# A hybrid decoder layer on one core: the down-projection's split inputs in the activations' pool, the second norm's row asked for later

## The chip, the core and the metric

The kernel runs on one core of a Trainium2 chip. The core has TensorE (PE: matmuls, with weight loads on a sequencer row of their own, PEld), VectorE (DVE), ScalarE (ACT), GpSimd (POOL) and SyncE (SP), which run side by side and wait for each other by semaphores; 16 DMA engines move data between HBM and the on-chip buffer. The metric is the device time of the one launch in microseconds; the median of three runs before is 2255.06 (2254.88 to 2256.31).

## The reference

One layer of a decoder trunk, sequence 512, model width 2048, feed-forward width 6144, everything in fp32. After an RMSNorm one input projection feeds three groups of heads (a pooling mixer, a gated DeltaNet, an RG-LRU); their outputs are joined and projected. What matters here is what follows:

```python
x = x + mixed @ w_out                       # 2048 x 2048
h = rmsnorm(x, norm2_w)
up = h @ w_up                               # 2048 x 12288
gate, val = jnp.split(up, 2, axis=-1)
gate = causal_dwconv(gate, conv_w)          # width 3
x = x + (jax.nn.gelu(gate) * val) @ w_down  # 6144 x 2048
return rmsnorm(x, final_norm_w)
```

`rmsnorm(x, w)` is `x * rsqrt(mean(x * x) + 1e-6) * w` over the 2048 features of a token.

## The kernel before

**Split products.** TensorE takes fp32 operands in a rounded form (`F32R`). To keep fp32 accuracy each operand is held as a rounded part `hi` and a rest `lo`, and each product is three matmuls into one sum: `hi*hi`, `hi*lo`, `lo*hi` (`mm3`, L198 to L203; so the three lines L201, L202 and L203 are the three passes). `parts` (L272) makes such a pair: a cast on ScalarE, a subtraction on VectorE. Activations lie feature by feature, 128 features on the partitions and the 512 tokens along the free axis, so they are the streamed operand; the weights (128x1024 fp32 a tile, 512 KB) come by DMA into `raw` and are split into `whi` and `wlo`.

**Two pools.** The pool `ap_` holds 32 tiles `ah0` to `al15` of 128x512 fp32: the split inputs `xh`, `xl` of the input projection (`ps_u`), then `yh`, `yl` of the out-projection (`ps_o`). As those are done, `act_tile` (L807) takes the tiles in turn from a list `free` for the up-projection. The pool `ep` of the feed-forward holds tags `r1` (two buffers), `r3`, `acc0` to `acc15`, and `ea0` to `ea11`.

**Up-projection.** The 2048 x 12288 product is done for each of 48 pairs of 128 gate and 128 value columns as a Strassen-like scheme: seven products (`b11`, `t1`, `b22`, `t2`, `b21`, `t3`, `t4`), each of 8 x 3 matmuls of 256 columns on one of seven *forms* of the activations. `fa` is the first form (a11: half of the features, half of the tokens; eight tiles made by `first_block`); `fb` holds two more; `fs` holds four sums of blocks (`split_sums`, L823: for six of the eight feature tiles in `ea0` to `ea11`, for the last two in tiles of `ap_`). The 336 products are sorted into slots; in slot n the weights of slot n + 3 are split, and loads run seven slots ahead. Weights of one chain are added up by DMAs on POOL's queue that accumulate onto the raw tile (L1172). The first slots are, in order: b11 of pair 0, b11 of pair 1, t1 of 0, b21 of 0, b22 of 0, t2 of 0, t1 of 1, t3 of 0. Sums are combined by ACT copies and DVE additions (`stage`, from L1199); `e` (L1213 after t2, L1217 after t3) is the DVE addition that reads bank `ps_y`, onto which the pair's next product in that bank writes.

**The second norm.** Its row of `1/rms` is not needed by the products, only by their results. The squares of the last out-projection features are added to `ssum` in slot 1 (`squares`, L866), and `last_squares` then spawns the coroutine `norm2`. A coroutine that yields a number is taken up again when the kernel's own count of PE's time, `now`, has moved on by so many microseconds; `token_rstd` (L160) first does four matmuls `ps_n` of `ssum` against ones, then a chain of 4-column operations on DVE (`ms_n` to `rt_n`, L170 and L130 to L135), yields 3.5, and then does four matmuls `n_ps` that spread the row over the partitions, and an ACT copy into `rstd` (L177).

**Down-projection.** The results `gelu(gate) * value` went to DRAM by pairs; `g_load` brings two of them back, `g_split` (L954) splits them into `gs` tiles. The 48 pairs are taken two at a time, each for two halves of the output features: a chunk is eight sums `ps_d` of 2 x 3 matmuls of 512 columns, each added to `accd` by DVE (L1007). The last two chunks are done by halves of 256 tokens (`ps_e`, L1086 and around), with the final norm's squares in 256-column tiles `sq3` (L1087) and the output's scaling after it.

**What sets the order.** From the end of the out-projection on, VectorE, ScalarE and GpSimd run in the order in which the code is written (`manual_schedule`); PE and SP do so everywhere. A tile of a tag waits for the last reader of the tile that lay there before.

`HK` = 8 is the number of feature tiles in half of the model width, `G` = 2 that of the inputs in a chunk.

Of the kernel before, what the change touches and what calls it, by code (L numbers as in the profile page):

```python
# [8 lines left out]
F32 = mybir.dt.float32  # L9
F32R = mybir.dt.float32r  # L10
# [8 lines left out]
P = 128  # L19
S = 512  # L20
# [42 lines left out]
G = 2  # L63
# [16 lines left out]
class Body:  # L80
# [704 lines left out]
    def out_phase(self):  # L785
        tc, nc, io = self.tc, self.nc, self.io
        with ExitStack() as ctx:
            pool = lambda name, **k: ctx.enter_context(tc.tile_pool(name=name, **k))
            g2 = pool("g2", bufs=1)
            ep = self.ep = pool("ffn", bufs=1)  # L790
# [3 lines left out]
            for p in range(HK):  # L794
                t = ep.tile([P, 2, S], F32, tag=f"acc{2 * p}", name=f"xp{p}")
# [6 lines left out]
            self.forms = {f: [None] * HK for f in BLOCKS + SUMS}  # L802
            free = [f"{t}{n}" for n in range(KT) for t in ("ah", "al")]
            tt = nc.vector.tensor_tensor
            st = {}

            def act_tile(name, shape):  # L807

                return self.ap_.tile(shape, F32R, tag=free.pop(0), name=name)

            def sums(p):

                big = p == HK - 1
                xs = ep.tile([P, 2, S], F32, tag="acc12" if big else "r3", name=f"xs{p}")
                for i in range(2):
                    nc.scalar.activation(xs[:, i, :], res(p + 8 * i), AF.Copy, scale=self.prm("n2", p + 8 * i))
                t = st[p] = ep.tile([P, 4, HT], F32, tag="acc8" if big else "r1", name=f"st{p}", bufs=1 if big else 2)
                a11, a21, a12, a22 = xs[:, 0, 0:HT], xs[:, 0, HT:S], xs[:, 1, 0:HT], xs[:, 1, HT:S]
                tt(out=t[:, 1, :], in0=a21, in1=a22, op=ALU.subtract)
                tt(out=t[:, 2, :], in0=t[:, 1, :], in1=a11, op=ALU.subtract)  # L820
                tt(out=t[:, 3, :], in0=t[:, 2, :], in1=a12, op=ALU.add)
                tt(out=t[:, 0, :], in0=a11, in1=a21, op=ALU.subtract)
# [17 lines left out]
            def split_block(x, h, l, d):  # L840
                nc.scalar.activation(h, x, AF.Copy, scale=self.prm("n2", d))
                nc.vector.scalar_tensor_tensor(out=l, in0=x, scalar=self.prm("n2", d), in1=h.bitcast(F32),
                                               op0=ALU.mult, op1=ALU.subtract)

            def first_block(p):
                t = act_tile(f"fa_{p}", [P, 2, HT])
                split_block(res(p)[:, 0:HT], t[:, 0, :], t[:, 1, :], p)
                self.forms["a11"][p] = t[:, 0, :], t[:, 1, :]
# [26 lines left out]
                        split_sums(d - HK)  # L875

            def norm2():
                yield 5.0
                yield from self.token_rstd(ssum, g2, "n2", rstd)

            for n in range(2):
# [39 lines left out]
            for i in range(2):  # L921
                out_done(DORD[KT - 2 + i], last[i])
            first_block(HK - 1)
            up.split(3)
            sums(HK - 1)
# [13 lines left out]
            gh, gl, wd, graw = {}, {}, {}, {}  # L939
# [9 lines left out]
            def g_load(j0):  # L949
                graw[j0] = ep.tile([P, G, S], F32, tag="r3", name=f"graw{j0}")  # L950
                for i in range(G):
                    nc.sync.dma_start(out=graw[j0][:, i, :], in_=up.gd[j0 + i])

            def g_split(j):  # L954
                j0, i = j // G * G, j % G
                odd = j0 // G % 2
                t = ep.tile([P, 2, S], F32R, tag=("r1", f"ea{i}")[odd], name=f"gs{j}", bufs=(2, 1)[odd])
                self.parts(graw[j0][:, i, :], t[:, 0, :], t[:, 1, :])
                gh[j], gl[j] = t[:, 0, :], t[:, 1, :]

            raws = {}

# [23 lines left out]
            for c, (j0, half) in enumerate(chunks[:-2]):  # L986
                ds = first[8 * (c % 2):8 * (c % 2) + 8] if c < 2 else range(8 * half, 8 * half + 8)
                for i, d in enumerate(ds):
# [11 lines left out]
                    pl, tag = (self.mm, "mm") if d % 2 else (self.aux, "aux")  # L1000
# [13 lines left out]
            j0 = NFF - G  # L1014
            wl = [wd[c - 1], wd[c]]
            HS = S // 2
# [1 line left out]
            s3 = g2.tile([P, 2, HS], F32, tag="ssum", name="ssum3")  # L1018
            r3 = g2.tile([P, 2, HS], F32, tag="rstd", name="rstd3")

            pts, norm_row = {}, {}
            AFTER = 9

            def sums(t, parts, last=False):
# [30 lines left out]
            def scale(t, e):  # L1055

                sl = slice(t * HS, (t + 1) * HS)
                a = acc[e][:, sl]
                if e < ND_:
                    nc.vector.scalar_tensor_tensor(out=a, in0=a, scalar=self.prm("nf", e), in1=norm_row[t][:, 0:HS],  # L1060
                                                   op0=ALU.mult, op1=ALU.mult)
                else:
                    nc.gpsimd.tensor_tensor(out=a, in0=a, in1=r3[:, t, :], op=ALU.mult)
                if e % 2:
                    nc.sync.dma_start(out=io["outT"][:, e - 1:e + 1, sl], in_=acc2[e // 2][:, :, sl])

            for t in range(2):
                sl = slice(t * HS, (t + 1) * HS)
                late, ps8, n8 = [], {}, 8 if t == 0 else 0

                def part(d, i):
                    hi, lo = wl[d // 8][i]
                    wsl = slice((d % 8) * P, (d % 8) * P + P)
                    self.mm3(ps8[d][:, :HS], hi, lo, wsl, gh[j0 + i][:, sl], gl[j0 + i][:, sl], i == 0, i == G - 1)
                    self.step(3 * T_R * HS / S)

                def parts(ds):
                    for d in ds:
                        pl, tag = (self.mm, "mm") if d % 2 else (self.aux, "aux")
                        ps8[d] = pl.tile([P, S], F32, tag=tag, name=f"ps_e{t}_{d}")  # L1080
                        part(d, 0)
                    for d in ds:
                        for i in range(1, G):
                            part(d, i)
                        a = acc[d][:, sl]
                        nc.vector.tensor_tensor(out=a, in0=a, in1=ps8[d][:, :HS], op=ALU.add)  # L1086
                        q = self.ap_.tile([P, HS], F32, tag=("ah", "al")[t] + str(d), name=f"sq3_{t}_{d}")  # L1087
                        if d == 0:
                            nc.scalar.activation(s3[:, t, :], a, AF.Square)
                            continue  # L1090
                        nc.scalar.activation(q, a, AF.Square)
                        if d < KT - NP[t]:
                            nc.gpsimd.tensor_tensor(out=s3[:, t, :], in0=s3[:, t, :], in1=q, op=ALU.add)
                        else:
                            late.append(q)
                            if len(late) > 2:
                                sums(t, late[-3:-2])
                        if t == 1 and d > AFTER:
                            self.ensure(lambda: 0 in norm_row)
                            scale(0, d - AFTER - 1)  # L1100
                            if d - AFTER - 1 + ND_ < KT:
                                scale(0, d - AFTER - 1 + ND_)

                if n8:
                    parts(range(n8))
                for d in range(n8, KT):
                    parts([d])
                if t == 1:
                    for e in range(KT - AFTER - 1, ND_):
                        scale(0, e)  # L1110
                self.spawn(finish(t, late))
# [197 lines left out]
```

## Time and profile before

| | before |
|---|---|
| median of three runs | 2255.06 us |
| profiled execution: time, span | 2254.35, 2252.6 us |
| PE busy | 2215.5 us (98%), 13998 matmuls |
| VectorE, ScalarE, GpSimd busy | 67%, 42%, 19% |
| mean granted TensorE clock | 0.993 |
| DMA | 340.01 MB, mean 151 GB/s |
| `ps_d` matmuls | three groups of 736, 394 ns each |
| PE waiting for `ssum` of the second norm | 2.6 us |

Busy time counts each matmul from its start to its modelled end, and consecutive matmuls overlap; so the mean duration of one (394 ns) is longer than the distance from one start to the next, and the distance is what sets the time where PE has no gap. It is read from starts in the timeline, or from the number of matmuls in a window.

In the span of 2252.6 us the input projection and the heads take the first part, the out-projection runs up to 741 us, the up-projection from 741 to 1694, the down-projection from there to the end. The granted clock is shown as a share of full speed: 1.00 is 2.4 GHz, 0.50 is the lower level of 1.2 GHz.

### The profile page before, as it was taken

Reading aid. Unit: us, or ns where it says so; the run is one execution under the profiler, and the core shown is the slowest. Engines: PE = TensorE matmul, PEld = TensorE weight load, DVE = VectorE, ACT = ScalarE, POOL = GpSimd, SP = SyncE. Lnnn points to the kernel's source line nnn. Section 1 sums busy time; section 2 is a strip of 40 time slices with the busy share of each in tenths; the row PEclk is TensorE's granted clock in tenths of the full one; section 3 lists DMA queues with packets and bytes.
Section 4 is the critical chain, followed back from the end, with each engine's and each line's share of the span. In section 5 each row is a group of like instructions: output and inputs, shape, how many; then the busy total and the mean of one; then the engine's idle time right before and its main releaser. Section 6 shows DMA issues by size and latency. Waiting matters only on the chain.

```text
span 2252.6 us, 35469 instructions
## 1 busy us (share of the span) xinstructions
PE 2215.5 (98%) x13998; PEld 1990.0 (88%) x13998; DVE 1520.4 (67%) x2340; ACT 943.9 (42%) x1371; POOL 437.9 (19%) x531
## 2 busy tenths in 40 slices
PE   9999999999999999999999999999999999999997
PEld 6878878888888999999999999999997888888886
DVE  8756657665545767666676766667667777777776
ACT  6646455434334544444444444444442222222223
POOL 4370731810122111111111111111110000000004
PEclk9999999999999999999999999999999999999998
DMA  6231222223534788888888888888875333333333
GB/s 197 82 98 62 87 87 84 88 89 113 187 126 136 152 201 204 206 201 202 200 204 192 202 205 200 204 202 201 210 188 187 112 122 112 122 113 122 113 123 102
DMA packets 109208, 340.01 MB, mean 151 GB/s; under 512 B 12720, under 2 KB 19120, under 8 KB 109040
## 3 DMA queue, kind: packets, MB, share of 16 engines
q1 hardware_dynamic: 78576, 229.72, 29.8%
q0 software_dynamic: 30464, 108.02, 26.3%
q8 instruction: 110, 1.80, 0.3%
q14 instruction: 58, 0.48, 0.1%
HBM read 314.36 MB, written 23.33 MB: 150 GB/s over the span
## 4 chain that ended last, share of the span: by engine, by line
PE 88%; POOL 4%; DVE 3%; issue 2%; ACT 1%; DMA 1%; SPq 0%; POOLq 0%; ACTq 0%; DVEq 0%
PE ps_y L1187 18%; PE ps_x L1187 12%; PE ps_z L1187 12%; PE ps_d L201 8%; PE ps_d L202 8%; PE ps_d L203 8%; PE ps_u L201 4%; PE ps_u L202 4%; PE ps_u L203 4%; PE ps_o L203 3%; PE ps_o L202 3%; PE ps_o L201 3%; POOL tm L581 2%; POOL tl L583 2%; PE ps_yt L118 1%
## 5 line engine op out<-in xcount | busy, mean ns | idle before, releaser
L1007 DVE TENSOR_TENSOR accd<-accd,ps_d 128x512 f32<-128x512 f32 x368 | 252.0, 686 | 138.6 <-PE ps_d L203 137.6
L201 PE MATMUL ps_d<-gs,whi_d 128*128 128x512 f32 x736 | 290.0, 394 | 0.0
L202 PE MATMUL ps_d<-gs,whi_d 128*128 128x512 f32 x736 | 290.0, 394 | 0.0
L203 PE MATMUL ps_d<-gs,wlo_d 128*128 128x512 f32 x736 | 290.0, 394 | 0.0
L1187 PE MATMUL ps_y<-fs,hi_t 128*128 128x256 f32 x1536 | 269.7, 278 | 1.1 <-DVE e L1213 1.1
L274 ACT CAST whi_d<-raw_d 128x1024 fp32r<-128x1024 f32 x96 | 100.5, 1051 | 388.0 <-PE ps_d L202 366.4
L1169 DVE TENSOR_TENSOR lo_t<-ra,hi_t 128x1024 fp32r<-128x1024 f32 x144 | 176.2, 1223 | 112.5 <-ACT hi_t L1168 112.4
L201 PE MATMUL ps_u<-xh,hi_in 128*128 128x512 f32 x608 | 246.3, 405 | 0.0
L203 PE MATMUL ps_u<-xh,lo_in 128*128 128x512 f32 x608 | 238.5, 392 | 0.0
L202 PE MATMUL ps_u<-xl,hi_in 128*128 128x512 f32 x608 | 237.9, 391 | 0.0
L1172 POOL DMA_DIRECT2D ra<-in_w_up x144 | 126.2, 876 | 557.5 <-DVE lo_t L1169 456.1
L1187 PEld LDWEIGHTS ps_y<-fs,hi_t 128*128 128x128 f32 x1536 | 232.9, 188 | 1.3 <-ACT h L1230 1.3
L1187 PE MATMUL ps_y<-fs,lo_t 128*128 128x256 f32 x768 | 213.1, 277 | 0.0
L1168 ACT CAST hi_t<-ra 128x1024 fp32r<-128x1024 f32 x144 | 151.5, 1052 | 74.4 <-PE ps_y L1187 46.1
L203 PEld LDWEIGHTS ps_d<-gs,wlo_d 128*128 128x128 f32 x736 | 137.6, 187 | 34.2
L201 PEld LDWEIGHTS ps_d<-gs,whi_d 128*128 128x128 f32 x736 | 137.6, 187 | 34.1
L202 PEld LDWEIGHTS ps_d<-gs,whi_d 128*128 128x128 f32 x736 | 137.6, 187 | 33.9
L189 DVE TENSOR_TENSOR lo_in<-raw_in,hi_in 128x1024 fp32r<-128x1024 f32 x80 | 104.4, 1307 | 78.0 <-ACT hi_in L188 77.4
L1187 PEld LDWEIGHTS ps_y<-fs,lo_t 128*128 128x128 f32 x768 | 144.3, 188 | 0.0
L1187 PE MATMUL ps_x<-fb,hi_b 128*128 128x256 f32 x768 | 141.4, 285 | 0.0
L1187 PE MATMUL ps_y<-fb,hi_t 128*128 128x256 f32 x768 | 140.1, 283 | 1.3 <-DVE e L1217 1.3
L1187 PE MATMUL ps_x<-fa,hi_b 128*128 128x256 f32 x768 | 140.0, 283 | 0.0
(357 smaller groups left out, 5109.4 us busy)
## 6 DMA issues: line engine op xcount, KB each, us to landing
ra<-in_w_up POOLq DMA_DIRECT2D x144, 512.0 KB, 7.8
raw_d<-in_w_down SPq DMA_DIRECT2D x96, 512.0 KB, 4.2
raw_in<-in_w_in SPq DMA_DIRECT2D x80, 512.0 KB, 3.7
ra<-in_w_up SPq DMA_DIRECT2D x48, 512.0 KB, 7.0
rc<-in_w_up SPq DMA_DIRECT2D x48, 512.0 KB, 6.5
rb<-in_w_up SPq DMA_DIRECT2D x48, 512.0 KB, 7.3
rb<-in_w_up POOLq DMA_DIRECT2D x48, 512.0 KB, 7.3
raw_o<-in_w_out SPq DMA_DIRECT2D x32, 512.0 KB, 3.8
```

The costliest lines, as they stand in the source:

```text
L189: nc.vector.tensor_tensor(out=lo, in0=raw, in1=hi.bitcast(F32), op=ALU.subtract)
L201: nc.tensor.matmul(ps, hi[:, sl], a, start=start, stop=False)
L202: nc.tensor.matmul(ps, hi[:, sl], b, start=False, stop=False)
L203: nc.tensor.matmul(ps, lo[:, sl], a, start=False, stop=stop)
L274: self.nc.scalar.copy(out=hi, in_=x)
L581: nc.gpsimd.tensor_tensor(out=t, in0=bc(ll[:, j, j + 1:32], j + 1), in1=tl[:, j:j + 1, 0:j + 1].broadcast_to([32, m, j + 1]), op=ALU.mult)
L583: nc.gpsimd.tensor_tensor(out=tl[:, j + 1:32, 0:j + 1], in0=tl[:, j + 1:32, 0:j + 1], in1=t, op=ALU.subtract)
L1007: nc.vector.tensor_tensor(out=acc[d], in0=acc[d], in1=ps, op=ALU.add)
L1168: nc.scalar.copy(out=hi, in_=raw)
L1169: nc.vector.tensor_tensor(out=lo, in0=raw, in1=hi.bitcast(F32), op=ALU.subtract)
L1172: nc.gpsimd.dma_start(out=raw, in_=self.block(j, self.NEXT[f]), accum_op=ALU.add)
L1187: mm = lambda w, x, s, e: nc.tensor.matmul(ps, w[:, sl], x, start=s, stop=e, skip_group_check=True)
```

## The change

The `gs` tiles of the down-projection (hi and lo side by side in one tile, alternately in `r1` and in `ea0`, `ea1`) become two separate tiles `gh` and `gl` in the activations' pool. They take the tags in which the first form's tiles `fa_0` to `fa_7` lay: `first_block` notes each tag, and `g_tags` gives two of them to each of four split inputs, for two pairs in turn. The `sq3` tiles of the final norm, which were in `ah` and `al` tags of that pool, go four at a time into `ea0` to `ea7`. And `norm2` yields 12.0 in place of 5.0 before it asks for the row.

```diff
@@ -802,7 +802,7 @@
             tt = nc.vector.tensor_tensor
-            st = {}
+            st, first_tags = {}, []
@@ -843,6 +843,7 @@
             def first_block(p):
+                first_tags.append(free[0])
                 t = act_tile(f"fa_{p}", [P, 2, HT])
@@ -875,7 +876,7 @@
             def norm2():
-                yield 5.0
+                yield 12.0
                 yield from self.token_rstd(ssum, g2, "n2", rstd)
@@ -951,12 +952,14 @@
+            g_tags = [[first_tags[4 * q + 2 * i:4 * q + 2 * i + 2] for i in range(G)] for q in range(2)]
             def g_split(j):
                 j0, i = j // G * G, j % G
-                odd = j0 // G % 2
-                t = ep.tile([P, 2, S], F32R, tag=("r1", f"ea{i}")[odd], name=f"gs{j}", bufs=(2, 1)[odd])
-                self.parts(graw[j0][:, i, :], t[:, 0, :], t[:, 1, :])
-                gh[j], gl[j] = t[:, 0, :], t[:, 1, :]
+                h, l = (self.ap_.tile([P, S], F32R, tag=t, name=f"g{k}{j}") for k, t in zip("hl", g_tags[j0 // G % 2][i]))
+                self.parts(graw[j0][:, i, :], h, l)
+                gh[j], gl[j] = h, l
@@ -1018,7 +1021,7 @@
-            pts, norm_row = {}, {}
+            pts, norm_row, sq4 = {}, {}, {}
             AFTER = 9
@@ -1084,7 +1087,10 @@
                         nc.vector.tensor_tensor(out=a, in0=a, in1=ps8[d][:, :HS], op=ALU.add)
-                        q = self.ap_.tile([P, HS], F32, tag=("ah", "al")[t] + str(d), name=f"sq3_{t}_{d}")
+                        if d % 4 == 0:
+                            q4 = ep.tile([P, 4, HS], F32, tag=f"ea{4 * t + d // 4}", name=f"sq3_{t}_{d}")
+                            sq4[t] = q4
+                        q = sq4[t][:, d % 4, :]
                         if d == 0:
```

In the built program a partition's bytes 65,248 to 130,783 are the activations' pool. The inputs in `gs` lay at 167,840 (`r1`) and from 180,128 on (`ea0`, `ea1`); `gh` and `gl` now start at 73,440, 79,584, 85,728, 91,872, 98,016, 104,160, 110,304 and 116,448. Addresses of everything else, the weights among it, are what they were.

PE's order at the second norm, before: the end of slot 2 (t1 of pair 0, into bank `ps_z`), the four `ps_n` matmuls, the start of slot 3 (b21 of pair 0).

```order
L1187 MATMUL ps_z_6502<-fs_7_0_6414,hi_t_0_6401 128x256
L1187 MATMUL ps_z_6502<-fs_7_0_6415,hi_t_0_6401 128x256
L1187 MATMUL ps_z_6502<-fs_7_0_6414,lo_t_0_6402 128x256
L167 MATMUL ps_n_6527<-cst,ssum_5337 128x1 x4
L1187 MATMUL ps_x_6430<-fb_0_6266,hi_b_0_6426 128x256
L1187 MATMUL ps_x_6430<-fb_0_6267,hi_b_0_6426 128x256
L1187 MATMUL ps_x_6430<-fb_0_6266,lo_b_0_6427 128x256
```

After: the `ps_n` matmuls stand between slot 5 (t2 of pair 0, into `ps_y`) and slot 6 (t1 of pair 1).

```order
L1193 MATMUL ps_y_6596<-fs_7_1_6418,hi_t_0_6497 128x256
L1193 MATMUL ps_y_6596<-fs_7_1_6419,hi_t_0_6497 128x256
L1193 MATMUL ps_y_6596<-fs_7_1_6418,lo_t_0_6498 128x256
L167 MATMUL ps_n_6621<-cst,ssum_5337 128x1 x4
L1193 MATMUL ps_z_6648<-fs_0_5355,hi_t_1_6530 128x256
L1193 MATMUL ps_z_6648<-fs_0_5356,hi_t_1_6530 128x256
L1193 MATMUL ps_z_6648<-fs_0_5355,lo_t_1_6531 128x256
```

The row's matmuls moved three slots down; the four `n_ps` matmuls, which are not shown, move from behind slot 4 to behind slot 7.

VectorE's order there, before: the end of the norm's chain, then the splits of weights (`lo_t_1` of pair 1's t1, `lo_t_0` of pair 0's t3 from the raw tile `rb`, `lo_b_1` of pair 1's b22), then `e` after t2 of pair 0.

```order
L134 TENSOR_TENSOR n_t<-n_t,ms_n_6532 128x4
L135 SCALAR_TENSOR_TENSOR rt_n_6534<-n_t,n_y 128x4
L1169 TENSOR_TENSOR lo_t_1_6552<-ra_6251,hi_t_1_6551 128x1024
L1169 TENSOR_TENSOR lo_t_0_6583<-rb_6255,hi_t_0_6582 128x1024
L1169 TENSOR_TENSOR lo_b_1_6619<-rb_6457,hi_b_1_6618 128x1024
L1213 TENSOR_TENSOR e_6455<-e_6455,ps_y_6623 128x256
```

After, from `ssum`'s last addition on:

```order
L867 TENSOR_TENSOR ssum_5337<-ssum_5337,sq_6467 128x512
L1175 TENSOR_TENSOR lo_t_0_6498<-ra_6249,hi_t_0_6497 128x1024
L1175 TENSOR_TENSOR lo_t_1_6531<-ra_6251,hi_t_1_6530 128x1024
L1175 TENSOR_TENSOR lo_t_0_6562<-rb_6255,hi_t_0_6561 128x1024
L1175 TENSOR_TENSOR lo_b_1_6592<-rb_6457,hi_b_1_6591 128x1024
L170 TENSOR_SCALAR ms_n_6626<-ps_n_6621 128x4
L130 TENSOR_SCALAR n_t<-ms_n_6626 128x4
```

```order
L133 SCALAR_TENSOR_TENSOR n_t<-n_y 128x4
L134 TENSOR_TENSOR n_t<-n_t,ms_n_6626 128x4
L135 SCALAR_TENSOR_TENSOR rt_n_6628<-n_t,n_y 128x4
L1219 TENSOR_TENSOR e_6455<-e_6455,ps_y_6596 128x256
L1220 TENSOR_TENSOR gv_6559<-ps_z_6502,e_6455 128x256
```

The three splits are now ahead of the norm's chain (`ms_n` to `rt_n`, of which the first and the last part are shown), and `e` follows directly behind it. ScalarE's copy into `rstd` comes later by as much; the orders on GpSimd and SP are the same.

PE's order where the down-projection begins, after; before, the streamed operand in each of these rows was a `gs` tile.

```order
L201 MATMUL ps_d_12_17461<-gh_17385,whi_d_0_17352 128x512
L202 MATMUL ps_d_12_17461<-gl_17386,whi_d_0_17352 128x512
L203 MATMUL ps_d_12_17461<-gh_17385,wlo_d_0_17353 128x512
L201 MATMUL ps_d_12_17461<-gh_17420,whi_d_1_17389 128x512
L202 MATMUL ps_d_12_17461<-gl_17421,whi_d_1_17389 128x512
L203 MATMUL ps_d_12_17461<-gh_17420,wlo_d_1_17390 128x512
```

Nothing moved there: the same matmuls with the same weights, on other tiles.

## Rows read from the trace of the kernel before

**Rows 1.** The page: span, and part 1, busy us of each engine.

```profile
span 2252.6 us, 35469 instructions
PE 2215.5 (98%) x13998; PEld 1990.0 (88%) x13998; DVE 1520.4 (67%) x2340; ACT 943.9 (42%) x1371; POOL 437.9 (19%) x531
```

**Rows 2.** Windows: length, PE, PEld, DVE, ACT, POOL busy, clock, DMA share, GB/s.

```profile
600.00:700.00 100.00, 100.00 (x443) 82.81 (x442) 45.13 (x51) 34.96 (x43) 22.11 (x20) 1.00 0.38 126
...
1740.00:2200.00 460.00, 460.00 (x1973) 368.63 (x1973) 332.88 (x454) 109.01 (x125) 0.00 (x0) 1.00 0.36 118
```

**Rows 3.** Groups of instructions of PE: count, busy us, mean ns, idle before.

```profile
L201 PE MATMUL ps_d<-gs,whi_d 128*128 128x512 f32 x736 | 290.0, 394 | 0.0
...
L201 PE MATMUL ps_o<-yh,hi_o 128*128 128x512 f32 x256 | 99.6, 389 | 0.0
...
L201 PE MATMUL ps_e<-gs,whi_d 128*128 128x256 f32 x64 | 18.2, 284 | 0.0
```

**Rows 4.** Timeline of PE in the up-projection: start us, us to the end.

```profile
989.65 0.39 PE L1187 MATMUL ps_z<-fs,hi_b 128*128 128x256 f32 x2
...
989.99 0.39 PE L1187 MATMUL ps_z<-fs,hi_b 128*128 128x256 f32 x2
...
991.38 0.40 PE L1187 MATMUL ps_x<-fa,hi_b 128*128 128x256 f32 x2
...
994.25 0.40 PE L1187 MATMUL ps_y<-fs,hi_t 128*128 128x256 f32 x2
```

**Rows 5.** Waits of PE: waiting, releaser: us in all, how many, longest.

```profile
PE ps_n L167 <- DVE ssum L866: 2.6, 1, 2.6
...
PE ps_y L1187 <- DVE e L1217: 1.3, 1, 1.3
...
PE ps_y L1187 <- DVE e L1213: 1.1, 1, 1.1
```

**Rows 6.** Timeline of DVE in the last half of the tokens.

```profile
2229.72 1.74 DVE L1086 TENSOR_TENSOR accd<-accd,ps_e 128x256 f32<-128x256 f32 x5
```

**Rows 7.** Timeline of DVE and PE at the third chunk's first matmul.

```profile
1714.52 1.22 DVE L275 TENSOR_TENSOR wlo_d<-raw_d,whi_d 128x1024 fp32r<-128x1024 f32 x1
...
1716.73 0.39 PE L201 MATMUL ps_d<-gs,whi_d 128*128 128x512 f32 x1
```

**Rows 8.** Timeline of PE at the second norm; in brackets the wait before.

```profile
749.04 0.28 PE L1187 MATMUL ps_z<-fs,lo_t 128*128 128x256 f32 x1
751.95 1.05 PE L167 MATMUL ps_n<-cst,ssum 128*128 128x1 f32 x8 [2.63 <-DVE ssum L866]
752.87 0.48 PE L1187 MATMUL ps_x<-fb,hi_b 128*128 128x256 f32 x2
...
757.23 0.48 PE L1187 MATMUL ps_z<-fs,hi_b 128*128 128x256 f32 x2
```

**Rows 9.** Windows behind the second norm's wait and at the up-projection's end.

```profile
754.00:756.00 2.00, 2.00 (x12) 2.00 (x11) 1.69 (x11) 0.00 (x0) 0.83 (x1) 0.50 1.07 207
...
1680.00:1740.00 60.00, 57.60 (x295) 48.21 (x295) 45.90 (x64) 19.40 (x25) 0.00 (x0) 1.00 0.59 190
```

**Rows 10.** Timeline of DVE, ACT and POOL at the second norm.

```profile
750.42 1.48 DVE L866 TENSOR_TENSOR ssum<-ssum,sq 128x512 f32<-128x512 f32 x2
...
753.59 0.16 DVE L170 TENSOR_SCALAR ms_n<-ps_n 128x4 f32<-128x4 f32 x1
...
755.84 1.23 DVE L1169 TENSOR_TENSOR lo_t<-ra,hi_t 128x1024 fp32r<-128x1024 f32 x1
...
763.94 0.42 DVE L1213 TENSOR_TENSOR e<-e,ps_y 128x256 f32<-128x256 f32 x1
...
757.73 1.05 ACT L1168 CAST hi_t<-rb 128x1024 fp32r<-128x1024 f32 x1
...
751.06 0.89 POOL L1172 DMA_DIRECT2D rb<-in_w_up  x1 [6.26 <-DVE lo_b L1169]
```

**Rows 11.** DMA issues of 750.5 to 751.5: count, KB each, us to landing.

```profile
rb<-in_w_up POOLq DMA_DIRECT2D x1, 512.0 KB, 5.7
```

## The prediction

> **What bounds the kernel.** First the header and the table by stage: TensorE (PE) is busy without a gap through the out-projection and the whole down-projection [rows 1, 2], so there an engine beside it can only lose time, and a microsecond is won only if PE's own matmuls come closer together. So the next thing read is their spacing. Of the matmuls that a window counts, one or two only reach into it; 100 us hold 441.5 starts in the out-projection, 226.5 ns each, and 460 us hold 1971.5 in the down-projection, 233.3 ns each [rows 2]. Both are 512 columns wide, in three passes (hi·hi, hi·lo, lo·hi), with weights from the same tiles `whi` and `wlo`, at full granted clock. The grouped rows say the same: 394 ns for one against 389 [rows 3].
>
> What differs is where the streamed operand lies. The out-projection streams `yh`, `yl` from the activations' pool (`ah0` to `al15`, in the built program bytes 65,248 to 130,783 of a partition); the down-projection streams `gs` from the tags `r1` (167,840) and `ea0`, `ea1` (180,128). That place matters shows inside one stage too. In the up-projection, 256 columns wide, a triple on `fs` in the `ea` tiles takes 989.99 - 989.65 = 0.34 us, while the eight triples of one product on `fa` in the activations' pool take 994.25 - 991.38 = 2.87, so 0.36 each [rows 4]. The sign turns with the width: the activations' pool gives 120 ns at 256 columns and 226.5 at 512, the other pool 113.3 and 233.3. I take these as four measured prices, without a mechanism.
>
> Third, PE's waits: ssum of the second norm 2.6 us, and two of 1.3 and 1.1 where the up-projection ends [rows 5]. The rest of PE's idle time lies in the first 180 us and at the very end, where nothing is moved.
>
> **The change, part by part.** *The split inputs move.* 2208 matmuls (three groups of 736 [rows 3]) read `gh`, `gl` from eight tiles of the activations' pool in which `yh` and `yl` lay in the out-projection, streamed 512 wide. I price them as those: 233.3 - 226.6 = 6.7 ns each, 14.7 us less. The bounds: at best this; at worst the pool's price at 256 columns doubled, 240 ns, which is 14.7 us more. The value taken is that of the same width in the same bytes.
> The Trainium skill speaks against it: "TensorE: Matmul & The Clock Gate", section Back-to-back issue gap, gives the spacing by the number of columns alone (an estimate from its formula is 215.8 ns for 512), and "SBUF — State Buffer", section Who interferes with whom, has TensorE wait on nobody for its operands. By that rule the move gives nothing; the two spacings for one width [rows 2] disagree with it.
>
> The last two blocks are done in halves of 256 columns: 192 matmuls (three groups of 64 [rows 3]) go from 113.3 to 120 ns, 1.3 us more. In the first half PE sets the pace, so its 96 x 6.7 ns = 0.64 us count in full. In the second DVE has five sums queued behind the norm's chain [rows 6], so I count 0.3 of the other 0.64. Together +0.9 (bounds 0.6 and 1.3).
>
> Do the other engines keep up? A chunk of 48 matmuls shrinks from 11.2 to 10.9 us. DVE is busy 332.9 of 460 us and ACT 109.0 [rows 2]; at the new pace DVE's share is 332.9/446.9 = 74%. The tightest place is the third chunk: its last `wlo` ends at 1714.52 + 1.22 = 1715.74 and PE starts it at 1716.73 [rows 7], 1.0 us to spare. Sixteen sums of six matmuls before it shorten by 16 x 0.04 = 0.64, so it holds; if its transfers do not follow, up to 0.6 us come back.
> The waits of the new tiles cost nothing: a `gh` waits for the last product on `fa`, which is b11 of the last block, nine slots or some 25 us (9 x 2.8) before the first split. That cover is wide.
>
> *The squares of the last norm* go to four-wide `ea` tiles, idle by then: same engines, same order, no added wait, 0.
>
> *The second norm's row.* Now PE starts slot 2's last matmul at 749.04 and could start the next one spacing, 0.12, later, at 749.16; it stands until 751.95, does the four `ps_n` matmuls, and starts slot 3 at 752.87 [rows 8]. Slot 3 then takes 757.23 - 752.87 = 4.36 us where such a slot takes 2.87 [rows 4]: after the stall the granted clock is 0.50, the lower level, 1.2 GHz [rows 9]. So the early request costs 2.79 + 1.49 = 4.28 us; the matmuls themselves (0.92) stay wherever they are put.
> Asked for after slot 5, ssum is long done (750.42 + 1.48 = 751.90 [rows 10]). But DVE now does `lo_t_1`, `lo_t_0` of `rb` and `lo_b_1` ahead of the norm's chain, and slot 7 (t3) adds onto the bank that `e` must read first; `e` stands behind the chain. Without stalls slot 3 on `fb` takes 2.87 and slots 4 to 6 on `fs` 2.77 each (six triples of 0.34 in `ea` tiles, two of 0.36 in the activations' pool): slot 5 ends at 757.57, `ps_n` at 758.5, slot 6 at 761.3. DVE: `rb`'s accumulating transfer is issued at 751.06 and lands 5.7 us later, 756.8 [rows 10, 11]; its cast takes 1.05 and the split 1.23 [rows 10], so `lo_t_0` runs from 757.85 to 759.08 and `lo_b_1`, whose operands are there, to 760.25. The chain lasts 755.84 - 753.59 = 2.25 [rows 10], to 762.5; `e` adds 0.42 [rows 10] and its signal 0.05 (as from ssum's end, 751.90, to `ps_n` at 751.95): slot 7 starts at 762.95, 1.65 us late. Today that landing is hidden behind the slow slot 3. The new wait is bounded by 0 (the transfer lands earlier) and, with the clock falling once more, 1.65 + 1.5. I take 1.65 without the fall: stalls of 1.1 and 1.3 us, 4 us apart, at the end of the up-projection left the granted clock at 1.00 [rows 5, 9]. Gain 4.28 - 1.65 = 2.6 us (bounds 1.1 and 4.3). ACT copies `rstd` after slot 7, 0.6 us ahead of a cast that PE needs three slots later: nothing. POOL and SP keep their orders.
>
> **Sum**, on the profiled execution (2254.35 us, span 2252.6): -14.7 + 0.9 - 2.6 = -16.4, so 2237.95. The median shown is 0.71 above that execution, which gives 2238.7.
>
> **Rivals.** (a) *The spacing belongs to the stage, not the place* (sums of only six matmuls, two inputs in turn), which is also what the skill's rule amounts to. Then only the norm pays: 2254.35 - 2.6 + 0.71 = 2252.5. For it: all 2208 have the one spacing, in `r1` and in `ea` tiles alike. Against it: one slot shows two spacings as its operand's place changes [rows 4]. Chance 0.09.
> (b) *Slower: the first form's tiles are slow in themselves.* Their 120 ns at 256 columns becomes 240 at 512: 2254.35 + 14.7 + 1.3 - 2.6 + 0.71 = 2268.5. It is slower than before from about 236 ns on, where 2208 x 2.8 ns outweigh the norm's gain and the 0.2%. For it: `fa` is the slower form [rows 4]. Against it: `yh` at 226.5 in the same bytes. Chance 0.03.
> (c) *The quicker PE runs into its suppliers*: weights or DVE late at each chunk, half of the gain back, 2238.7 + 7.4 = 2246. For it: the 1.0 us at the third chunk [rows 7]. Against it: PE has no gap in 460 us and DVE a quarter of the time free. Chance 0.05.
>
> **How the numbers follow.** The forecast has 0.83. Its own range, from the bounds of its terms (norm -4.3 to -1.1, halves +0.6 to +1.3, third chunk 0 to 0.6), is 2236.7 to 2241.2. The range given reaches down by the scatter of the three runs, to 2236, and up to 2246, to take in half of (c); (a) and (b) are outside. A run of this kernel tells 0.2%, 4.5 us, from no change: faster holds the forecast and (c), 0.88; same is (a), 0.09; slower (b), 0.03.
>
> **What would show it.** In the profile after: `ps_d` matmuls 226.5 ns apart, some 2030 in 460 us of the down-projection and 389 ns for one; `ps_e` 120 ns apart in the first half; no wait of `ps_n` on ssum; about 1.7 us of PE waiting for DVE's `e` at the first block's t3; granted clock 1.00 around it. An unchanged 233 ns with those waits gone would mean (a), 240 (b), and 226.5 with PE gaps at the chunks' starts (c).

## The result, and the profile after

The changed kernel takes 2237.21 us (median of four runs, 2235.93 to 2238.1) against 2254.97 for the kernel before (four runs): 0.992 of it, 95% interval 0.9902 to 0.9937. The prediction was 2238.7, range 2236 to 2246.

The page of after, the span and part 1 (busy us, share, instructions), and then two windows (length, busy us and count of PE, PEld, DVE, ACT, POOL, granted clock, DMA share, GB/s):

```profile
span 2235.3 us, 35469 instructions
PE 2199.9 (98%) x13998; PEld 1991.0 (89%) x13998; DVE 1517.4 (68%) x2340; ACT 944.6 (42%) x1371; POOL 437.6 (20%) x531
```

```profile
600.00:700.00 100.00, 100.00 (x443) 82.81 (x442) 45.18 (x51) 34.97 (x43) 22.01 (x20) 1.00 0.40 126
...
1740.00:2200.00 460.00, 460.00 (x2064) 382.31 (x2063) 343.09 (x472) 113.85 (x134) 3.27 (x5) 1.00 0.36 118
```

The out-projection is as in [rows 2]. The window that held 1973 matmuls of the down-projection now holds 2064; the last 8 us of it already belong to the 256-column halves. In the groups of PE (count, busy us, mean ns) `ps_d` now has the duration of `ps_o`, 389 ns, where [rows 3] had 394, and `ps_e` has gone the other way, 284 to 289:

```profile
L201 PE MATMUL ps_d<-gh,whi_d 128*128 128x512 f32 x736 | 286.3, 389 | 0.0
...
L201 PE MATMUL ps_o<-yh,hi_o 128*128 128x512 f32 x256 | 99.6, 389 | 0.0
...
L201 PE MATMUL ps_e<-gh,whi_d 128*128 128x256 f32 x64 | 18.5, 289 | 0.0
```

At the second norm, the timeline of PE (start, us, in brackets the wait before) and of DVE and ACT:

```profile
757.70 0.95 PE L167 MATMUL ps_n<-cst,ssum 128*128 128x1 f32 x8
763.04 0.47 PE L1193 MATMUL ps_y<-fs,hi_t 128*128 128x256 f32 x2 [1.52 <-DVE e L1219]
```

```profile
757.95 1.23 DVE L1175 TENSOR_TENSOR lo_t<-rb,hi_t 128x1024 fp32r<-128x1024 f32 x1 [3.73 <-ACT hi_t L1174]
759.10 1.22 DVE L1175 TENSOR_TENSOR lo_b<-rb,hi_b 128x1024 fp32r<-128x1024 f32 x1
760.23 0.15 DVE L170 TENSOR_SCALAR ms_n<-ps_n 128x4 f32<-128x4 f32 x1
...
762.48 0.41 DVE L1219 TENSOR_TENSOR e<-e,ps_y 128x256 f32<-128x256 f32 x1
...
756.87 1.05 ACT L1174 CAST hi_t<-rb 128x1024 fp32r<-128x1024 f32 x1 [3.64 <-DMA rb<-in_w_up]
```

`ps_n` waits for nothing any more ([rows 8] had 2.63 us). The transfer into `rb` has landed when its cast begins at 756.87; then come the split, the split of `lo_b`, the norm's chain, `e`, and slot 7 of the up-projection, 1.52 us late at 763.04. The window behind that stall has full clock, where [rows 9] had 0.50:

```profile
763.00:765.00 2.00, 1.96 (x16) 1.99 (x17) 2.00 (x3) 0.00 (x0) 0.00 (x0) 1.00 0.99 217
```

Matmul by matmul the two traces can be laid side by side, as the order of PE's big products is the same. What after has gained (-) or lost in each stretch, from the starts of the matmuls at its ends:

| stretch | measured, us | predicted |
|---|---|---|
| up to the up-projection | +0.05 | 0 |
| its slots 0 to 19 (the second norm) | -2.38 | -2.6 |
| slots 20 to 332 | 0.00 | 0 |
| slot 333 (a wait for `e`) | -0.84 | 0 |
| 2208 `ps_d` matmuls | -14.70 | -14.7 |
| `ps_e`, first half of the tokens | +0.62 | +0.64 |
| `ps_e`, second half, to the end | 0.0 | +0.3 |
| span | -17.3 | -16.4 |

### The profile page after: what moved, and what is told of

Same layout as the page of the kernel before. It is cut to its first block, busy times and chain, and to the rows that moved or that the text cites. A ratio compares the mean times of both kernels' runs of the same rounds, so it can differ in the third digit from the quotient of the medians.

```text
span 2235.3 us, 35469 instructions
## 1 busy us (share of the span) xinstructions
PE 2199.9 (98%) x13998; PEld 1991.0 (89%) x13998; DVE 1517.4 (68%) x2340; ACT 944.6 (42%) x1371; POOL 437.6 (20%) x531
## 4 chain that ended last, share of the span: by engine, by line
PE 85%; POOL 5%; DVE 4%; issue 2%; ACT 2%; DMA 2%; SPq 0%; POOLq 0%; ACTq 0%; DVEq 0%
PE ps_y L1193 17%; PE ps_x L1193 12%; PE ps_z L1193 11%; PE ps_d L203 7%; PE ps_d L201 7%; PE ps_d L202 7%; PE ps_u L201 3%; PE ps_u L202 3%; PE ps_u L203 3%; PE ps_o L202 3%; PE ps_o L201 3%; PE ps_o L203 3%; POOL tm L581 2%; POOL tl L583 2%; DVE lo_in L189 1%
## 5 line engine op out<-in xcount | busy, mean ns | idle before, releaser
L201 PE MATMUL ps_d<-gh,whi_d 128*128 128x512 f32 x736 | 286.3, 389 | 0.0
L202 PE MATMUL ps_d<-gl,whi_d 128*128 128x512 f32 x736 | 286.3, 389 | 0.0
L203 PE MATMUL ps_d<-gh,wlo_d 128*128 128x512 f32 x736 | 286.3, 389 | 0.0
L1193 PEld LDWEIGHTS ps_y<-fs,hi_t 128*128 128x128 f32 x1536 | 233.1, 188 | 2.2 <-ACT hi_b L1174 1.7
L202 PEld LDWEIGHTS ps_d<-gl,whi_d 128*128 128x128 f32 x736 | 138.1, 188 | 28.8
L203 PEld LDWEIGHTS ps_d<-gh,wlo_d 128*128 128x128 f32 x736 | 138.1, 188 | 28.6
L201 PEld LDWEIGHTS ps_d<-gh,whi_d 128*128 128x128 f32 x736 | 138.1, 188 | 28.6
```

Of the source, the lines that this page charges most:

```text
L201: nc.tensor.matmul(ps, hi[:, sl], a, start=start, stop=False)
L202: nc.tensor.matmul(ps, hi[:, sl], b, start=False, stop=False)
L203: nc.tensor.matmul(ps, lo[:, sl], a, start=False, stop=stop)
L1193: mm = lambda w, x, s, e: nc.tensor.matmul(ps, w[:, sl], x, start=s, stop=e, skip_group_check=True)
```

## The experiments

The kernel before was run beside each group of kernels; its medians there were 2253.85 (for e1, e2, e3), 2254.97 (e4, v1, v2), 2253.98 (w1, w2), 2253.82 (w3) and 2252.96 (w4). One trace was kept of each kernel.

**The two parts alone.** e1 is before with `yield 12.0`; e2 is after with `yield 5.0`.

```diff
-                yield 5.0
+                yield 12.0
```

> Before, with only the second norm's row asked for later (12.0 in place of 5.0); the split inputs stay where they were. If the two parts of the change add up, this gives what slots 3 to 8 gave in the trace of after: 2.4 us less than before, 2252.6, with ps_d matmuls 233.3 ns apart, no wait of ps_n on ssum and about 1.5 us of PE waiting for e at the first t3. The stall of 1.1 us on e at the end of the up-projection, which is gone in after, should still be there if the move of the split inputs took it away, and be gone or other if it is scatter of a transfer. Rival: the two stalls of 1.5 us or the later clock cost as much as the early request did; then no gain, 2255.

> After, with the second norm's row asked for as early as before (5.0). If the parts add up: 14.7 us less for 2208 matmuls 226.6 ns apart, 0.6 more for the first 96 matmuls of ps_e, so 2254.97 - 14.1 = 2240.9, and up to 0.8 less where the stall on e at the end of the up-projection goes with it, 2240.1; ps_n waits 2.6 us for ssum as before. Rival: the spacing would also have come with the norm alone (a different state of PE); then 2255.

e1: 2250.39, ratio 0.9985 (0.9976 to 0.9994). e2: 2239.08, ratio 0.9939 (0.9925 to 0.9953). Laid beside before, e1's trace gains 2.87 us in slots 0 to 19 and nothing in the down-projection (another 2.1 us lie before the out-projection begins, where it has the instructions of before; I take them as scatter); e2's gains 14.70 in `ps_d` and 0.00 in slots 0 to 19, and loses 0.62 in `ps_e`. The parts add up, to within 0.5 us: the 2.87 of e1 against the 2.38 of after follow the landing of `rb` at the second norm, which came 5.3 us after its issue in e1 and 5.8 in after. The same window of both shows it in its count, 1973 of before against 2049 (e2's runs on into the halves for less time than after's):

```profile
1740.00:2200.00 460.00, 460.00 (x1973) 368.67 (x1972) 333.13 (x453) 105.69 (x122) 0.00 (x0) 1.00 0.34 117
```

```profile
1740.00:2200.00 460.00, 460.00 (x2049) 381.82 (x2048) 342.42 (x468) 111.05 (x130) 0.00 (x0) 1.00 0.35 119
```

The wait at the end of the up-projection answers to neither part. PE's waits there, of e1 (old tiles) and of e2 (new tiles):

```profile
PE ps_y L1187 <- DVE e L1213: 1.4, 1, 1.4
```

```profile
PE ps_y L1193 <- DVE e L1219: 1.0, 1, 1.0
```

Before had 1.1 [rows 5], after 0.3, the kernel e4, further on, 0.8. What the wait follows is the last transfer that accumulates into `rb`. It is issued 10.8 us before slot 333 in before and in after alike; it lands 8.1 us later in before, 7.2 in after, 8.4 in e1 and 7.9 in e2, and the cast behind it starts the chain that ends with `e`. That cast, of before and then of after (slot 333 begins at 1682.93 and 1680.61):

```profile
1680.26 1.05 ACT L1168 CAST hi_t<-rb 128x1024 fp32r<-128x1024 f32 x1 [3.26 <-PE ps_z L1187]
```

```profile
1677.10 1.05 ACT L1174 CAST hi_t<-rb 128x1024 fp32r<-128x1024 f32 x1 [2.45 <-DMA rb<-in_w_up]
```

It begins 2.67 us ahead of slot 333 in before and 3.51 in after: the 0.84 us of the table. Why this transfer takes longer in one trace than in another is not shown; neither part of the change goes with it.

**Is it the place, or the address?** e3 is before with 64 idle bytes ahead of everything in the feed-forward's pool.

```diff
             ep = self.ep = pool("ffn", bufs=1)
+            pad = ep.tile([P, 16], F32, name="pad")
+            nc.gpsimd.memset(pad, 0.0)
```

> Before, with one idle tile of 64 bytes a partition at the head of the feed-forward's pool, so that r1, ea0 to ea11 and all else there start 64 bytes later (bytes 96 past a multiple of 128, as the activations' pool does, in place of 32); pools, tags and order are those of before. Theory 1, the start address within its line sets the spacing: ps_d on gs falls from 233.3 to 226.7 ns (2208 x 6.7 = 14.7 us less), the products on fs in ea tiles rise from 113.3 to 120 ns (192 slots x 18 = 3456 x 6.7 = 23.2 us more), ps_e rises by 1.3 at most: 2255 - 14.7 + 23.2 + 0.6 to 1.3 = 2264.1 to 2264.8. Theory 2, the region of the buffer (low bytes of the activations' pool against those above 160,000) sets it: nothing changes, 2255, 233.3 and 113.3 ns.

2260.37, ratio 1.0035 (1.0022 to 1.0049): 6.5 us slower, where 9 were expected. `gs`, still in `r1` and `ea`, has the spacing of the activations' pool, and `fs` in `ea` too (timeline of e3: triples at 992.42, 992.78, and so on, 0.36 apart to `fs_7`, where [rows 4] had 0.34):

```profile
L201 PE MATMUL ps_d<-gs,whi_d 128*128 128x512 f32 x736 | 286.3, 389 | 0.0
```

```profile
992.42 0.40 PE L1189 MATMUL ps_z<-fs,hi_b 128*128 128x256 f32 x2
992.78 0.40 PE L1189 MATMUL ps_z<-fs,hi_b 128*128 128x256 f32 x2
```

In the trace `ps_d` gains 14.7 us, slots 8 to 332 lose 22.3, `ps_e` 0.6; gained besides are 1.3 us of the scattering wait, 1.0 in the norm's stretch and 0.4 ahead of it. The 1.0 goes with the clock: `ps_n` waited 2.5 us here too, but the granted clock stayed at 1.00, where [rows 9] had 0.50. The region is refuted: 64 bytes do it.

**Spacing by address, by itself.** m1 and m2 do no layer, only runs of 48 matmuls (hi, hi, lo) on one tile.

```diff
+for n, (c, o, q) in enumerate(RUNS):     # columns, byte of the operand, byte of the weights
+    for k in range(16):
+        for j in range(3):
+            nc.tensor.matmul(ps[:, :c], w[:, j // 2, q // 4 + (k % 8) * P:...],
+                             mv[:, o // 4 + (0, 1024, 0)[j]:...], ...)
```

> Not the layer: only runs of 48 matmuls (hi, hi, lo in turn, weight loads as in mm3) on one streamed tile, which start 0, 16, 32 ... 240 and a few other bytes past a multiple of 256, each once with 512 and once with 256 columns; nothing is computed from the result. Theory 1 (address in its line): 512 columns take 233.3 ns at 32 and 160 bytes and 226.7 at 96 and 224, 256 columns 113.3 at 32 and 160 and 120 at 96 and 224, and 288 reads like 32, 480 like 96; other offsets may give still other spacings. Theory 2 (region or pool): one spacing for each width at all offsets.

> Not the layer: runs of 48 matmuls as in the first such measurement, now for each pair of a byte at which the streamed operand starts (0, 32, ... 224 past a multiple of 256) and a byte at which the weights start (the same eight), each with 512 and with 256 columns; nothing is computed from the result. Theory 1a, the two reads get in each other's way, so their offset to each other sets the spacing: 226.7 and 120 ns wherever operand and weights start at the same byte of 256 (as with 224 and 224 before), 233.3 and 113.3 where the operand starts 64 bytes ahead of the weights. Theory 1b, the operand's own start sets it: each column of operands' bytes has the spacing that it had with the weights at 224 (228.9 and 113.3 ns at 32, 233.3 and 113.3 at 160, 226.7 and 120 at 224), whatever the weights' start.

In m1 the weights start at 224 bytes past a multiple of 256, and the numbers are the operand's starting byte and the ns from start to start in the settled part of a run (its last 30). It has 226.7 and 120.0 (512 and 256 columns) at 224 and 480, and 233.3 and 113.3 at 160, which are the kernel's pairs; but 232.3 and 118.7 at 96, so the period is 256 bytes, not 128. At 32 and 288 it has 228.9 and 113.3, though at 544, the same byte modulo 256, 233.3 and 117.8. Of 16 starts in steps of 16 bytes none was below 226.7 or 113.3. In m2 the table of eight by eight repeats along its diagonals: the offset, the operand's start minus the weights', decides, as theory 1a has it. That the two reads get in each other's way, the reason that 1a gives, is not shown by it.

```
operand minus weights (mod 256 bytes)    0     32     64     96    128    160    192    224
512 columns, ns (lowest of eight)    226.7  233.3  228.9  233.3  232.2  234.1  233.3  233.3
 (the highest of eight)              226.7  233.4  228.9  233.3  233.3  234.5  233.4  233.4
256 columns, ns (lowest of eight)    120.0  116.6  113.3  120.0  118.6  117.3  113.3  118.3
 (the highest of eight)              120.0  116.7  117.8  120.0  120.0  118.7  117.8  118.4
```

The end of its timeline, where each row is one run and the weights start at 224: `ps_fa`, 512 columns at offset 0, takes 1124.94 - 1114.05 = 10.89 us for 48, 226.9 each with its first, unsettled ones; `ps_ey`, 512 at offset 224, 1108.36 - 1097.17 = 11.19, 233.1; `ps_ez`, 256 at offset 224, 5.69, 118.5.

```profile
1097.17 11.35 PE L120 MATMUL ps_ey<-mv,w 128*128 128x512 f32 x48
1108.36 5.85 PE L120 MATMUL ps_ez<-mv,w 128*128 128x256 f32 x48
1114.05 11.06 PE L120 MATMUL ps_fa<-mv,w 128*128 128x512 f32 x48
1124.94 5.91 PE L120 MATMUL ps_fb<-mv,w 128*128 128x256 f32 x48
```

In before all weights start at 224, the activations' pool at 224 (offset 0), the feed-forward's at 160 (offset 192). With 256 columns, offsets 64 and 192 show two values, 113.3 and 117.8, and no third (seven and five of the eight at 113.3); w1 shows what that means. The 512 columns at byte 544 of m1, 233.3 ns where the same offset has 228.9 everywhere else, stay unexplained.

**Three cuts at what is left.** All three start from after. e4 asks for the row after slot 3; v1 puts the activations' pool 64 bytes on (offset 64) and keeps the feed-forward's pool where it was; v2 is both.

```diff
-                yield 12.0
+                yield 7.0                                               # e4, v2
+            self.pad = [self.ap_.tile([P, 16], F32, name="pad0")]       # v1, v2, ahead of the pool's tiles
```

> After, with the row asked for after slot 3 (7.0) in place of after slot 5 (12.0). If the stall of 1.5 us at the first t3 comes from e standing behind the norm's chain, which itself stands behind the split of rb, it goes: the chain now stands ahead of that split, ps_n is reached at about 752.0, just when ssum is done (751.9), so PE waits at most 0.1 us for either; 1.5 us less than after, 2235.7 where after is 2237.2. Rival: slot 7's weights themselves (the landing of rb at 756.8, its cast and split to 759.1) or ssum bind PE as much; then a stall of about 1 to 1.5 us stands elsewhere and the time is that of after.

> After, with an idle tile of 64 bytes a partition ahead of the activations' pool, so that all operands there start 64 bytes (modulo 256) past the weights, and with the feed-forward's pool where it was (four small tiles of the last norm lie in ea8 to ea11 to make the room). Theory 1a, the offset of operand to weights: 512 columns go from 226.7 to 228.9 ns (608 x 3 + 256 x 3 + 736 x 3 = 4800 matmuls, 10.6 us more), the 4608 of 256 columns on fa, fb and the last two fs go from 120 to 113.3 (30.7 us less), the first half of ps_e too (0.6 less): 20.7 us less than after, 2216.5 where after is 2237.2. Theory 1b, the operand's own start (32 past a multiple of 256, weights at 224): the same numbers, since both measurements agree there. Theory 2, the pool: as after, 2237. A limit that is not in PE, weights that come late when a slot takes 2.7 in place of 2.88 us (DMA 0.6 to 0.9 busy in that stage): between the two, with PE waiting for hi and lo tiles.

> The two edits together: the activations' pool 64 bytes ahead, and the row asked for after slot 3. If they add up: 20.7 + 1.5 less than after, 2215.0. Rival: with slots of 2.72 us in place of 2.87 ssum comes late for ps_n (slots 2 and 3 end 0.3 us earlier), and 0.3 to 0.5 of the 1.5 us come back as a wait of ps_n on ssum, after which the clock may be lower: 2215.5 to 2217.

e4: 2235.87, ratio to before 0.9910 (0.9896 to 0.9923), its stall at slot 7 gone: against after's trace slots 0 to 19 gain 1.98 us, and `ps_n` starts at 751.93, one spacing behind slot 3 and 0.2 us behind ssum. Of this 1.0 is lost again before the down-projection, half of it at one product (slot 314) and half in the wait for `e`; the medians are 1.3 us apart. v2: 2234.01, ratio 0.9908 (0.9895 to 0.9922). v1: 2236.27, ratio 0.9915 (0.9902 to 0.9929), where 2216.5 was expected. The 512-column spacing came as forecast (`ps_d` 228.9), but `fa` and `fb` settled at 117.8 in place of 113.3 (24 matmuls of each product, mean), so 4608 x 2.0 = 9 us came in where 30.7 were expected. In its trace, against after's, the up-projection is 8.2 us shorter (its wait for `e` is 1.0 longer), `ps_o` and `ps_d` are 6.6 us longer and the first half of `ps_e` 0.6 shorter. That half, on the same bytes in both, was at 113.3 ns in v1 and at 117.8 in v2.

**Weights moved instead.** w1 is after with the weights in one tile (in a pool opened behind the activations', no longer ahead of it), 64 bytes further on in the up-projection alone, so that all its operands have offset 192; w2 adds the row after slot 3; w3 is w2 with the shift from slot 12 on.

```diff
-            hi = wp.tile([P, 1024], F32R, tag="whi", name=f"hi_{f}_{j}", bufs=NW)
-            lo = wp.tile([P, 1024], F32R, tag="wlo", name=f"lo_{f}_{j}", bufs=NW)
+            hi, lo = self.b.weights(16)      # columns of W, 16 ahead; w3: 16 if self.n_split > 12 else 0
```

> After, with the split weights in one tile (four hi and four lo places in turn, as before) that has 64 bytes to spare: in the up-projection they lie 64 bytes further on than in the other stages. The activations' pool stays at 224 past a multiple of 256, the feed-forward's pool comes to 224 too, so in the up-projection every operand starts 192 bytes (modulo 256) past its weights, elsewhere 0. Theory 1a, offset of operand to weights: 512 columns keep 226.7 ns; the 144 products on fa and fb go from 119.75 to 113.3 ns (144 x 24 x 6.4 = 22.2 us), the 192 on fs from 115.1, their mean now, to 113.3 (192 x 24 x 1.8 = 8.4 us): 30.6 less than after, 2206.6 where after is 2237.2. Theory 1b, the operand's own start: fa and fb keep 119.75, fs rises to 120 (22 us more): 2259. Rival, the suppliers: slots of 2.72 us need weights 5% faster where the DMA engines are busy 0.8 to 0.9; then PE waits for hi and lo tiles and part of the 30 us comes back, 2207 to 2225.

> The same, and the second norm's row asked for after slot 3 (7.0): 1.5 us less again, 2205.1. Rival: slots 2 and 3 are 0.2 us shorter, so ps_n comes to ssum some 0.2 to 0.4 us early and waits; 2205.5.

> The kernel of the run before this (weights 64 bytes further on in the up-projection, row after slot 3), but the first twelve products of the up-projection still have their weights where the other stages have them, so that they run at offset 0 (120 ns) and offset 192 begins with the thirteenth. Theory 1c, offset 192 holds either of two rhythms, 113.3 or 117.8 ns, and the one into which a product comes is kept: entered from the 120 ns of offset 0, as every product on fs is in before and after, it is 113.3, and all 324 products keep it: 12 x 24 x 6.7 = 1.9 us more than the 2205.1 forecast for the all-113.3 kernel, 2207; one execution of that kernel took 2207.3 and the others 2239 to 2242. Rival: what decides is not the entry but each product's own operand, and 117.8 comes back within some slots: 2239 to 2241, or between, by the number of slots that keep 113.3.

In w1 and w2 the last product of the up-projection works with 16 columns of weights that the next tile has already overwritten, and in w3 those of slots 9 to 11 do too; the count and shape of the instructions is not changed by it. w1: 2240.48. w2: seven runs at 2238.6 to 2242.0 and one at 2207.34. Operands whose own start modulo 256 had not moved (`fa`, `fb`) went from 119.8 to 117.8, so 1b, the operand's own start, is refuted a second time. The timeline of w1, merged by product, shows both rhythms at one offset: the product that starts at 754.19 is over at 756.91, 2.72 us or 113.3 ns a matmul; that at 767.88 takes 2.83, 117.8, and so do the 324 behind it, up to the waits at the up-projection's end. Between them stand fp32 matmuls and a wait:

```profile
754.19 2.88 PE L1195 MATMUL ps_y<-fs,W 128*128 128x256 f32 x24
756.91 0.95 PE L167 MATMUL ps_n<-cst,ssum 128*128 128x1 f32 x8
757.72 3.07 PE L1195 MATMUL ps_z<-fs,W 128*128 128x256 f32 x24
761.34 2.98 PE L1195 MATMUL ps_y<-fs,W 128*128 128x256 f32 x24 [0.55 <-ACT e L1217]
764.16 1.05 PE L118 MATMUL n_ps<-cst,rt_n 128*128 128x128 f32 x8
764.97 3.07 PE L1195 MATMUL ps_z<-fs,W 128*128 128x256 f32 x24
767.88 2.99 PE L1195 MATMUL ps_y<-fb,W 128*128 128x256 f32 x24
770.71 2.99 PE L1195 MATMUL ps_x<-fa,W 128*128 128x256 f32 x24
```

w3 (2251.76, one run of twelve at 2219.66) did not test what it was made for: the change of place made PE wait in slots 9 to 11, in part at the lower clock (213 ns a matmul), and the shift was not entered from a steady 120. After that it ran at 117.8 until one short disturbance at 1643, behind which 20 products took 113.3, until the wait for `e`.

**Two offsets in turn.** w4, which asks for the row after slot 3 as well, lets hi and lo alternate in the tile, so that nothing is overwritten early, and puts the feed-forward's pool at 96: `fa`, `fb` and the last two `fs` have offset 192, the other `fs` 64.

```diff
+        return (self.W[:, a:a + 1024] for a in (2048 * n + ahead, 2048 * n + 1024 + ahead))
-                ms = g2.tile([P, n], F32, tag=f"ms{n}", name=f"ms3_{t}", bufs=2)
+                ms = ep.tile([P, n], F32, tag=f"ea{8 + t}", name=f"ms3_{t}")
```

> After, with the row asked for after slot 3, the up-projection's weights 64 bytes further on (hi and lo places in turn in one tile, so that nothing of one product's weights is overwritten before it is read), and the feed-forward's pool at 96 past a multiple of 256: in the up-projection fa, fb and the last two fs start 192 bytes past their weights, the other six fs 64 past, so that operands of two offsets follow each other in every product on fs; 512 columns stay at offset 0. Theory 1c, at 192 the rhythm is that into which the matmuls come, and coming from another offset it is 113.3: 144 products on fa and fb go from 119.75 to 113.3 (22.2 us less), the 192 on fs from 115.1 to 116.9 (18 at 117.8, 6 at some 114; 8.1 us more), 14.1 us less than the same kernel with its operands as in after, which took 2235.9: 2221.8. Rival: fa and fb fall back to 117.8 as in the two kernels with one offset: 6.8 us less for them, 10 to 12 more for fs: 2239 to 2241.

Both, in turn: 2222.39, 2241.82, 2222.39, 2241.79, 2239.76, 2223.30. The profiled execution is one of the quick ones (span 2220.6); its timeline, merged by product, has 1006.07 - 1003.35 = 2.72 us for `fa` (113.3 ns) and 2.81 for `fs` (117.1; 116.9 is the mean of 178 products), as expected:

```profile
1003.35 2.88 PE L1195 MATMUL ps_x<-fa,W 128*128 128x256 f32 x24
1006.07 2.97 PE L1195 MATMUL ps_y<-fs,W 128*128 128x256 f32 x24
1008.88 2.88 PE L1195 MATMUL ps_x<-fb,W 128*128 128x256 f32 x24
```

No trace of one of the others was kept. An estimate from the two spacings fits them: with `fa` and `fb` (113.3 in the trace) and the last two `fs` (114.5) at 117.8, 144 x 24 x 4.5 ns + 192 x 6 x 3.3 ns = 19 us more, where the runs lie 16 to 19 apart. So w4's best executions are 15 us quicker than after and its others 3 to 5 slower. The version that beats both kernels in every run is v2 (2233.6 to 2234.6), by 3 us.

## Why the prediction was right

*The spacing.* All of 14.7 us came from the price that the prediction read off `yh` [rows 2], 226.7 ns measured over the 2208 starts where 226.6 was taken. The price was right for a reason that the prediction did not have: what counts is the start of the operand against that of its weights, modulo 256 bytes, and the activations' pool and the weights happen to have the same. The pool that the prediction named is not the cause: in e3 the other pool had this price, in v1 the activations' pool had another. "The same width in the same bytes" was enough only because the weights stayed in theirs; w1 moved the weights and the same start had another price. Rival (a), the stage, is refuted by the trace of after and again by e3; (b), the doubled 256-column price, by after; (c), late suppliers, by the third chunk: the first three chunks each gained 0.30 to 0.32 us, nothing came back. The Trainium skill, "TensorE: Matmul & The Clock Gate", section Back-to-back issue gap, has its formula by the number of columns alone for the isolated matmul, and says that in a stream with weight loads both set the spacing, which the prediction left out. The rows of m2 agree in that the weights count: for 512 columns they have 226.7 to 234.5 ns, by where the operand lies against its weights.

*The halves.* +0.62 in the first, as worked out. In the second the 0.3 did not come: from there to the end it is 32.1 us in before and in after, so the dearer matmuls cost nothing, as DVE's queue of sums [rows 6] lets expect. That term was too big by 0.3.

*The second norm.* The prediction had slot 7 start at 762.95 and be 1.65 us late; it started at 763.04, 1.52 us late, and every link of the chain (landing, cast, split, `lo_b`, chain, `e`) stood within 0.2 us of its place. The clock did not fall behind it, as the prediction had taken. The gain was 2.38 in after and 2.87 in e1, around the 2.6. Of the 4.28 us that the early request was said to cost, 1.49 are the lower clock behind the wait, and not every execution has that: e2 waited 2.6 us and had 0.50 from 755 to 758 us, e3 waited 2.5 and had 1.00 in every window from 752 to 770. e4 shows that the new stall was the order's doing: asked for two slots earlier the chain fits into DVE's wait for `rb`, and slots 0 to 19 are 2.0 us shorter.

*What was not foreseen.* 0.84 us of a wait for `e` at the up-projection's end, which lies between 0 (e3) and 1.4 us (e1) in the traces, by the landing of a transfer. That this fell in after's favour is luck. The forecast of 16.4 and the 17.3 measured in the profile differ by this, by the 0.3 of the halves and by 0.2 of the norm with the other sign.

What stays open is why an offset has the spacing that it has, and what settles which of the two rhythms an execution falls into. The runs show only that a rhythm is kept from product to product and that a disturbance can switch it either way (w1, w3). Coming from offset 0 does not settle it: in w1 and w4 the first `fa`, right behind `ps_o` at offset 0, took 117.8.

## What to carry to other kernels

Where PE is busy without a gap, measure the distance from start to start for each pair of tiles; if one width has two, look at the start addresses of operand and weights before looking for an engine to blame. A price read at the same width, the same operand bytes and the same weights' bytes carried over to 0.1 ns; the pool or the operand's bytes alone did not (v1, w1). A request that makes PE wait should be placed by what stands behind it in the other engines' order too: two slots were worth 2 us where they lie, and 1.3 us of the median.

## What the runs showed of the hardware

- Matmuls of 512 columns with a weight load each started 226.7 to 234.5 ns apart, those of 256 columns 113.3 to 120, at full granted clock, by the offset of operand to weights modulo 256 bytes (m2). No single offset is best for both: 0 gives 226.7 and 120, 64 gives 228.9 (233.3 in one run of m1) and 113.3 or 117.8.
- At offsets 64 and 192, matmuls of 256 columns have two steady spacings, 113.3 and 117.8 ns. One kernel, w4, took 2222 or 2241 us from run to run; that its slow runs are the 117.8 fits by size and is not shown by a trace. In the layouts of before and after this costs next to nothing: `fs` at offset 192 comes from offset 0 in each product and settled at 113.3 in all 178 of slots 20 to 329. Only behind a wait or the fp32 matmuls of the norm it did not always: in after the `ea` tiles of slots 7, 8 and 334 took 117.8, with slot 11, the next on `fs`, back at 113.3; in before, where slot 334 waited 1.1 us, none did. Offset 0 has one spacing.
- Waits of 2.6 us before matmuls were followed by some microseconds at a granted clock of 0.50 in before [rows 8, 9] and in e2; one of 2.5 us in e3 and one of 1.5 us in after were not. The length of the wait alone does not tell it here.
